# GpSimd's low halves of the weights: one subtraction over 512 columns, or two over 256

## The chip, the cores and the metric

The kernel runs on one NeuronCore of a Trainium2 chip. The metric is device microseconds for one execution, lower is better. Three runs of the kernel before took 1372.89, 1378.55 and 1378.11 us; the median is 1378.11 us. The profile is of one further execution.

## The reference

One sequence of 512 tokens with 1024 features goes through two different layers, all in float32.

- The first layer projects the normalised tokens with one wide matrix `w_in` into the inputs of three branches and three gates. Branch A is attention that keeps for each query 128 keys chosen by an index score; branch B is a gated linear recurrence (`hgrn2`); branch C is attention over compressed keys and values with rotary parts (`mla`). Each branch is projected up, gated, summed, projected by `w_out` and added to x. A feed-forward block with 2816 hidden columns follows: `x + (silu(h @ w_ffn_gate) * (h @ w_ffn_up)) @ w_ffn_down`, and a norm.
- The second layer scales and shifts its normalised input by a vector made from `c @ w_ada`, projects it with a second `w_in`, runs sparse attention of two branches with compressed keys beside them, and a state-space scan (`s5`), and adds the projected result to x.

Nearly all arithmetic is products of the tokens with weight matrices. Each weight is used once, so each is brought in from memory once per execution.

## The kernel before, in words

**Weights in two halves.** TensorE multiplies in a rounded float32. To keep full precision each operand is kept as two tiles, a high half (the value rounded) and a low half (what the rounding left), and one product is three matmuls: high by high, high by low, low by high. That is `mm3` (L176 to L179), and its three lines lead the profile. The halves of the activations are made by `split` (L181): a cast on ScalarE and a subtraction on VectorE. The halves of the weights are made by `wsplit` (L201): ScalarE casts the raw weights to `whi` (L206), and GpSimd subtracts, `wlo = wraw - whi` (L207).

**One load.** `wraw` (L194) brings up to 1024 float32 columns on 128 partitions (512 KB) into one of three raw buffers; the transfer is issued by SyncE's queue (L198). `wsplit` handles a load in two pieces, each of half of the load's `kc` blocks of rows: mostly 512 columns each, but 256 for the half-size loads, 64 to 384 for a few others, and 656 for two. There are three `whi` and three `wlo` buffers too. A raw buffer comes free, and the next transfer into it may start, when GpSimd has finished with it. A `whi` buffer comes free when the last matmul and the subtraction have read it. `early` (L131) asks for the next load one step before the present one is used.

**Who reads the low halves.** Where the weights are TensorE's stationary operand (`proj_t`, `proj_g`) the low half is read at L178; where they are the moving one (`proj_tok`, `proj_tok_g`) at L179. No other line changes with the piece of the subtraction.

**What sets the order.** Each engine works through its own list in order, and semaphores hold an instruction until what it reads is there. In the first stage the lists of TensorE, VectorE and ScalarE are in the order in which the code writes them (`manual_schedule`, L497). In all other stages the framework's planner orders each engine's list when the program is built, from its own estimate of when each instruction could start; a few edges (`issue_after`) pin single groups behind others. The code itself interleaves work by generators: the `todo` queue (L104) and `turns` (L140) step projections between the pieces of attention, the scan and the norms. GpSimd's list holds the subtractions of L207, and among them a few other things: the softmax weights (L365), masks for branch A (L1060, L1061), two products of a rotary table (L1650, L1651), and sums near the end.

**VectorE's chains that the prediction follows.** `rsqrt_steps` (L271) is a chain of eleven tiny operations on a few columns (L279 to L290). `rope2` (L1643) turns a tile by a table; copies at L1700 and transposes at L1704 follow. In the feed-forward loop (L1400) an activation is gated at L1406 and L1408 and split at L188, and between them VectorE makes the tables of the state-space scan (`cmul`, L1098, by `tt`, L1095). L838 adds a gated product to `mixed`.

Of the kernel before, what the change touches and what calls it, by code (L numbers as in the profile page):

```python
# [19 lines left out]
OP = mybir.AluOpType  # L20
# [72 lines left out]
def fl(ap):  # L93
    return ap.bitcast(FT)
# [56 lines left out]
def tile_hybrid(ctx: ExitStack, tc: tile.TileContext, I, out):  # L151
    nc = tc.nc
# [37 lines left out]
    def wload(parts, kc, cols, dst=None):  # L190

        return wsplit(wraw(parts, kc, cols), kc, cols, dst)
# [8 lines left out]
    def wsplit(raw, kc, cols, dst=None):  # L201
        hi, lo = dst or [wp.tile([128, 1024], FR, tag=t_, bufs=3, name=t_) for t_ in ("whi", "wlo")]
        n = kc * cols
        for c in range(0, kc, (kc + 1) // 2):
            d = slice(c * cols, min(c + (kc + 1) // 2, kc) * cols)
            nc.scalar.copy(hi[:, d], raw[:, d])  # L206
            nc.gpsimd.tensor_tensor(lo[:, d], raw[:, d], fl(hi[:, d]), op=OP.subtract)  # L207
        return [x[:, :n].rearrange("p (k c) -> p k c", k=kc) for x in (hi, lo)]

    def wcols(w, c0, cols, kc=KD, k0=0):  # L210
# [286 lines left out]
    with tc.manual_schedule(engines={mybir.EngineType.DVE, mybir.EngineType.Activation, mybir.EngineType.PE}):  # L497
# [13 lines left out]
        def weights(k):  # L511
            w_first[k] = wsplit(raws[k], min(3, KD - k), 328)
# [53 lines left out]
        for c0, n in ((0, 512), (512, 128)):  # L566
            p = s_ps()
            nc.tensor.matmul(p[0:4, 0:n], rb, oh[:, c0:c0 + n], start=True, stop=True)
            nc.scalar.copy(byd[:, c0:c0 + n], p[0:4, 0:n])
        half(2, 4)  # L570
        wk = wsplit(raw_k, KD, 128, [pa.tile([128, 1024], FR, name=f"wik{i}") for i in range(2)])
        product(0, 6)
        product(1, 6)
# [1508 lines left out]
```

## Time and profile before

| | |
|---|---|
| Median of three runs | 1378.11 us |
| The profiled execution: its own time | 1378.97 us |
| The profiled execution: span from first to last instruction | 1377.2 us |
| TensorE busy | 1279.4 us (93%) |
| VectorE busy | 858.9 us (62%) |
| GpSimd busy | 640.1 us (46%), of it 507.1 us in the 388 subtractions into `wlo` |
| ScalarE busy | 551.5 us (40%) |
| Mean granted TensorE clock | 0.97 of full speed |

In the views PE is TensorE's matmuls, PEld its weight loads, DVE is VectorE, ACT is ScalarE, POOL is GpSimd and SP is SyncE; a q behind an engine's name means its sequencer. A tile's name stands as written<-read. A busy time counts overlapping instructions once. A wait is put down to the release that came last.

### The profile page before, as it was taken

How to read it: one execution, taken by the hardware profiler on the slowest of the kernel's cores; microseconds unless marked ns; L12 is line 12 of the kernel's file. 1: busy time of each engine (PE TensorE's matmuls, PEld its weight loads, DVE VectorE, ACT ScalarE, POOL GpSimd, SP SyncE). 2: the span in 40 equal slices, each digit the busy share in tenths (PEclk: the TensorE clock that was granted, in tenths of full speed). 3: DMA queues.
4: the chain of work that ended last, by engine and by line, in shares of the span. 5: the costliest groups of instructions: out<-in, count | busy, mean ns of one | idle time of the engine just before them, and what ended most of it. 6: DMA issues, size and time to landing. Idle time of an engine off the chain costs nothing. (4 is left out here: it accounts for less than half of the span.)

```text
span 1377.2 us, 18201 instructions
## 1 busy us (share of the span) xinstructions
PE 1279.4 (93%) x6418; PEld 1054.0 (77%) x6418; DVE 858.9 (62%) x1831; ACT 551.5 (40%) x1242; POOL 640.1 (46%) x552
## 2 busy tenths in 40 slices
PE   8989999999989999999998899999989788789998
PEld 6777887777768888878876688887778678677786
DVE  6755897776534346268667516354363758897885
ACT  4554542322234434343423123432343234447772
POOL 3334433333455455554565345554532443547663
PEclk9999999999999999999999899999999898999999
DMA  6252222221423373333765434533325665231233
GB/s 199 71 158 58 63 75 65 62 57 36 116 80 88 86 176 92 123 92 115 224 196 187 143 99 121 169 109 102 113 77 162 185 173 132 69 92 47 77 108 138
DMA packets 201962, 156.16 MB, mean 113 GB/s; under 512 B 27535, under 2 KB 175707, under 8 KB 201869
## 3 DMA queue, kind: packets, MB, share of 16 engines
q1 hardware_dynamic: 201868, 154.98, 38.7%
q8 instruction: 51, 0.84, 0.3%
q14 instruction: 43, 0.34, 0.1%
HBM read 136.58 MB, written 18.37 MB: 113 GB/s over the span
## 5 line engine op out<-in xcount | busy, mean ns | idle before, releaser
L207 POOL TENSOR_TENSOR wlo<-wraw,whi 128x512 fp32r<-128x512 f32 (+4 forms) x388 | 507.1, 1327 | 602.7 <-ACT whi L206 601.4
L206 ACT CAST whi<-wraw 128x512 fp32r<-128x512 f32 (+4 forms) x388 | 212.3, 575 | 366.1 <-issue 217.3
L177 PE MATMUL mm<-hT,whi 128*128 128x512 f32 (+2 forms) x840 | 335.8, 400 | 0.0
L179 PE MATMUL mm<-hT,wlo 128*128 128x512 f32 (+2 forms) x840 | 327.9, 390 | 0.0
L178 PE MATMUL mm<-hT,whi 128*128 128x512 f32 (+2 forms) x840 | 327.7, 390 | 0.0
L179 PEld LDWEIGHTS mm<-hT,wlo 128*128 128x128 f32 x840 | 160.4, 191 | 31.3
L177 PEld LDWEIGHTS mm<-hT,whi 128*128 128x128 f32 x840 | 160.9, 191 | 29.9 <-PE mm L179 0.5
L178 PEld LDWEIGHTS mm<-hT,whi 128*128 128x128 f32 x840 | 161.0, 192 | 28.5 <-issue 0.7
L177 PE MATMUL mm<-whi,gT 128*128 128x512 f32 x176 | 71.7, 408 | 14.5 <-DVE t2k L1406 6.9
L1225 DVE TENSOR_TENSOR XT<-XT,mm 128x512 f32<-128x512 f32 x24 | 16.3, 685 | 99.7 <-PE mm L179 99.6
L178 PE MATMUL mm<-wlo,gT 128*128 128x512 f32 x176 | 71.3, 405 | 0.0
L179 PE MATMUL mm<-whi,gT 128*128 128x512 f32 x176 | 71.2, 405 | 0.0
L177 PE MATMUL mm<-whi,hT 128*128 128x512 f32 (+3 forms) x160 | 60.1, 375 | 0.3 <-ACT hT L184 0.3
L179 PE MATMUL mm<-whi,hT 128*128 128x512 f32 (+3 forms) x160 | 59.3, 371 | 0.9 <-DVE hT L185 0.9
L178 PE MATMUL mm<-wlo,hT 128*128 128x512 f32 (+3 forms) x160 | 59.3, 371 | 0.2 <-POOL wlo L207 0.2
L1287 DVE SCALAR_TENSOR_TENSOR am<-aw,prm,am 128x1024 f32<-128x1024 f32 x21 | 32.4, 1543 | 36.2 <-DMA aw<-in_w_ada_dram 36.2
L185 DVE TENSOR_TENSOR pt4k<-tp,pt4k 128x512 fp32r<-128x512 f32 (+1 forms) x96 | 45.8, 483 | 14.4 <-ACT pt4k L184 13.7
L177 PEld LDWEIGHTS mm<-whi,gT 128*128 128x128 f32 x176 | 34.2, 194 | 24.7 <-DVE t2k L1406 7.3
L184 ACT CAST pt4k<-tp 128x512 fp32r<-128x512 f32 (+1 forms) x96 | 40.1, 421 | 32.0 <-PE tp L387 30.8
L187 ACT ACTIVATE gT<-t2k 128x512 fp32r<-128x512 f32 x22 | 13.9, 631 | 82.3 <-DVE t2k L1408 82.3
L179 PEld LDWEIGHTS mm<-whi,gT 128*128 128x128 f32 x176 | 34.1, 194 | 8.3
L178 PEld LDWEIGHTS mm<-wlo,gT 128*128 128x128 f32 x176 | 34.1, 194 | 7.9
(641 smaller groups left out, 2666.8 us busy)
## 6 DMA issues: line engine op xcount, KB each, us to landing
wraw<-in_w_in_dram SPq DMA_DIRECT2D x70, 512.0 KB
aw<-in_w_ada_dram SPq DMA_DIRECT2D x24, 512.0 KB
wraw<-in_w_ffn_gate_dram SPq DMA_DIRECT2D x22, 512.0 KB
wraw<-in_w_ffn_up_dram SPq DMA_DIRECT2D x22, 512.0 KB
wraw<-in_w_ffn_down_dram SPq DMA_DIRECT2D x20, 512.0 KB
wraw<-in_w_out_dram SPq DMA_DIRECT2D x16, 512.0 KB
PA<-biasd SPq DMA_DIRECT2D x4, 640.0 KB
x<-in_x_dram SPq DMA_DIRECT2D x4, 512.0 KB
```

The source lines that it names most:

```text
L177: nc.tensor.matmul(o, a[0], b[0], start=first, stop=False)
L178: nc.tensor.matmul(o, a[0], b[1], start=False, stop=False)
L179: nc.tensor.matmul(o, a[1], b[0], start=False, stop=last)
L184: nc.scalar.copy(hi, p)
L185: return nc.vector.tensor_tensor(lo, p, fl(hi), op=OP.subtract)
L187: nc.scalar.activation(hi, p, AF.Copy, scale=scale)
L206: nc.scalar.copy(hi[:, d], raw[:, d])
L207: nc.gpsimd.tensor_tensor(lo[:, d], raw[:, d], fl(hi[:, d]), op=OP.subtract)
L1225: nc.vector.tensor_tensor(XT[:, t, n0:n0 + 512], XT[:, t, n0:n0 + 512], o, op=OP.add)
L1287: nc.vector.scalar_tensor_tensor(am, aw, cs[:, k:k + 1], am, op0=OP.mult, op1=OP.add)
```

## The change

The subtraction of each piece is issued in parts of at most 256 columns. The cast on ScalarE keeps its size, and the values written are the same. A piece of 512 columns becomes two instructions on GpSimd, one of 384 becomes 256 and 128, one of 656 becomes three; pieces of 256 and less stay as they are.

```diff
         for c in range(0, kc, (kc + 1) // 2):
             d = slice(c * cols, min(c + (kc + 1) // 2, kc) * cols)
             nc.scalar.copy(hi[:, d], raw[:, d])
-            nc.gpsimd.tensor_tensor(lo[:, d], raw[:, d], fl(hi[:, d]), op=OP.subtract)
+
+            for e0 in range(d.start, d.stop, 256):
+                e = slice(e0, min(e0 + 256, d.stop))
+                nc.gpsimd.tensor_tensor(lo[:, e], raw[:, e], fl(hi[:, e]), op=OP.subtract)
         return [x[:, :n].rearrange("p (k c) -> p k c", k=kc) for x in (hi, lo)]
```

## Rows read from the trace of the kernel before

**Rows 1.** The page: span, busy time of each engine, and the chain that ended last.
```profile
span 1377.2 us, 18201 instructions
...
PE 1279.4 (93%) x6418; PEld 1054.0 (77%) x6418; DVE 858.9 (62%) x1831; ACT 551.5 (40%) x1242; POOL 640.1 (46%) x552
...
PE 17%; DVE 8%; issue 1%; ACT 1%; DMA 1%; POOL 0%; DVEq 0%; SPq 0%; ACTq 0%; POOLq 0%
```

**Rows 2.** TensorE's waits: who waited for whom: us in total, times, longest us.
```profile
PE tp L1040 <- DVE rq_y L290: 8.8, 4, 6.1
...
PE tp L1704 <- DVE t2k L1700: 7.4, 2, 4.2
PE mm L177 <- DVE t2k L1406: 6.9, 1, 6.9
...
PE s L1012 <- DVE bK L1021: 3.7, 4, 1.7
...
PE mm L179 <- POOL wlo L207: 1.4, 1, 1.4
...
PE s L408 <- DVE mn L354: 0.2, 1, 0.2
```

**Rows 3.** GpSimd's groups by shape: count, busy us, mean ns, idle before, releaser.
```profile
L207 POOL TENSOR_TENSOR wlo<-wraw,whi 128x512 fp32r<-128x512 f32 x301 | 431.1, 1453 | 464.5 <-ACT whi L206 464.2
...
L207 POOL TENSOR_TENSOR wik<-wraw,wik 128x512 fp32r<-128x512 f32 x2 | 2.5, 1290 | 5.1 <-ACT wik L206 5.1
...
L1651 POOL TENSOR_TENSOR t2k<-tok,tab 128x256 f32<-128x256 f32 x2 | 1.5, 730 | 0.0
```

**Rows 4.** VectorE's groups by shape, two of the same shape.
```profile
L838 DVE TENSOR_TENSOR mixed<-mixed,t2k 128x512 f32<-128x512 f32 x16 | 21.4, 1335 | 0.3
...
L837 DVE SCALAR_TENSOR_TENSOR t2k<-t2k,mm 128x512 f32<-128x512 f32 x16 | 11.0, 687 | 41.2 <-PE mm L179 39.8 <-ACT t2k L835 1.4
```

**Rows 5.** Timeline of VectorE and GpSimd near 101 us: start us, duration us, instruction.
```profile
101.31 0.16 DVE L290 SCALAR_TENSOR_TENSOR rq_y<-rq_u,rq_y 128x4 f32<-128x4 f32 x1
101.51 1.21 DVE L286 TENSOR_TENSOR rq_u<-rq_y 128x4 f32<-128x4 f32 x1
...
101.44 1.26 POOL L207 TENSOR_TENSOR wlo<-wraw,whi 128x512 fp32r<-128x512 f32 x1 [1.17 <-ACT whi L206]
```

**Rows 6.** The same near 261 us, where GpSimd's pieces have 256 columns.
```profile
260.78 0.70 DVE L290 SCALAR_TENSOR_TENSOR rq_y<-rq_u,rq_y 128x4 f32<-128x4 f32 x1
...
260.73 1.55 POOL L207 TENSOR_TENSOR wlo<-wraw,whi 128x256 fp32r<-128x256 f32 x2 [7.77 <-ACT whi L206]
```

**Rows 7.** The same from 1169 to 1177.5 us.
```profile
1170.86 1.51 DVE L1653 TENSOR_TENSOR tok<-tok,tab 128x256 f32<-128x256 f32 x1
...
1176.38 0.89 DVE L1700 COPY t2k<-tok 128x256 f32<-128x256 f32 x4
...
1170.62 5.69 POOL L207 TENSOR_TENSOR wlo<-wraw,whi 128x512 fp32r<-128x512 f32 x4
```

**Rows 8.** The same from 752 to 760.5 us.
```profile
757.58 1.24 DVE L1096 TENSOR_TENSOR t2k<-PH 128x8 f32<-128x8 f32 x1
...
759.36 0.68 DVE L1406 SCALAR_TENSOR_TENSOR t2k<-t2k,mm 128x512 f32<-128x512 f32 x1
...
751.62 7.17 POOL L207 TENSOR_TENSOR wlo<-wraw,whi 128x512 fp32r<-128x512 f32 x4 [4.31 <-ACT whi L206]
```

**Rows 9.** Waits of ScalarE and of SyncE's queue.
```profile
ACT whi L206 <- PE mm L178: 80.1, 39, 6.3
ACT whi L206 <- POOL wlo L207: 34.9, 18, 4.2
...
SPq L198 <- POOL wlo L207: 843.8, 165, 15.7
```

**Rows 10.** One stretch: busy us of PE, PEld, DVE, ACT, POOL; granted clock; DMA.
```profile
760.00:766.00 6.00, 2.68 (x6) 1.67 (x7) 5.79 (x27) 0.63 (x1) 0.00 (x0) 0.50 0.46 132
```

**Rows 11.** Timeline of GpSimd alone: two pieces of 512 columns back to back.
```profile
776.95 2.54 POOL L207 TENSOR_TENSOR wlo<-wraw,whi 128x512 fp32r<-128x512 f32 x2 [2.08 <-ACT whi L206]
```

## The prediction

> **What bounds the kernel now.** I read the page's busy times first: TensorE is busy 1279.4 of 1377.2 us, VectorE 62%, GpSimd 46% [rows 1]. So at most 98 us are idle on TensorE, and whatever the change does off TensorE is worth nothing until it touches those. The chain of waits agrees: TensorE 17% of the span, VectorE 8%, GpSimd 0% (the chain is followed back only part of the way) [rows 1]. Next, the list of TensorE's waits, to see who ends the idle time. The 26 entries of that list that VectorE ends run from 8.8 us down to 0.2 us [rows 2] and add up to 78 us; GpSimd's subtraction ends almost nothing directly, 1.4 us in its largest entry [rows 2]. The low halves are therefore early enough, and the question is whether GpSimd reaches TensorE by way of VectorE.
>
> It does. L838 and L837 are both 128x512 on VectorE; L837 reads PSUM (`mm`) and takes 687 ns, L838 reads two SBUF tiles and takes 1335 ns on the mean [rows 4]. The timeline shows why. At 101.31 us a step on 4 columns takes 0.16 us. The next begins at 101.51, just after a subtraction began at 101.44, and takes 1.21 us: it ends at 102.72, when the subtraction (to 102.70) is done [rows 5]. With pieces of 256 columns the same kind of step takes 0.70 us [rows 6]. So a VectorE operation on SBUF waits for the rest of the running subtraction, 1.21 − 0.16 = 1.05 us behind 512 columns and 0.54 behind 256.
>
> **The change part by part.**
>
> *The instructions.* 327 pieces have 512 columns: 301 into `wlo` [rows 3] and 26 into four other tiles. They become 654; the odd widths (384, 328, 280, 656) add 28 more. So GpSimd gets 355 more. An undisturbed subtraction of 512 columns takes 1290 ns; a two-input operation on 256 takes 730 [rows 3]. Two for one cost 2 × 730 − 1290 = 170 ns, over 327 pieces 56 us, and some 5 us for the odd ones: GpSimd goes from 640 to about 700 us, 51%. By spacing: two of 512 take 2.54 us together, 1.27 each [rows 11], two of 256 1.55 us with some waiting [rows 6], which gives 0 to 0.28 us per pair; I keep 0.17. The Trainium skill (Perfetto Trace Analysis, GPSIMD Engine Instruction) says to time GpSimd by the spacing of starts, since its spans don't compose; by the spacing with waits, 0.28, the added work would be 92 us, still below any engine's limit.
>
> *What hides it.* TensorE's work on a load hides the subtraction. The cast waits 80.1 us in 39 places for TensorE to free its buffer [rows 9], so in these places the weights run ahead by the depth of the buffers. If that cover is gone, a stall per load grows by two to four times 0.17. The next transfer is issued when GpSimd frees the raw buffer: SyncE waits 843.8 us for that, 165 times [rows 9], so each of these transfers goes out 0.3 us later, behind it in SyncE's queue everything else too. ScalarE waits for GpSimd 34.9 us, 18 times [rows 9]; with two late pieces each, 18 × 0.34 = 6 us, and behind the waiting cast stand the evictions that VectorE waits for. ScalarE is 40% busy, so I cost this at 0, with 6 us as the upper bound. TensorE may start a load after its first 256 columns of low half, which is worth at most the 1.4 us it waits now [rows 2]; I take 0.
>
> *What VectorE gains.* A single operation that meets a subtraction waits half as long: 0.5 us less behind a full piece, 0.25 on the mean. A chain of operations is another matter. VectorE and GpSimd then alternate, one instruction each, until the burst of subtractions is used up. I worked two chains that end in a stall.
>
> First, 1170.86 to 1176.38 us: four operations in step with four subtractions of 512, 5.52 / 4 = 1.38 us apart, then the copies, two of which release TensorE [rows 7]. With pieces of 256 the step shrinks by 1290 − 730 = 0.56 to 0.82 us, but eight pieces stand ahead, so the two copies queue as well: 6 × 0.82 = 4.9 us, against 5.52 plus some 0.4 for the copies. Gain: 1.0 of the 4.2 us stall [rows 2].
>
> Second, the stall of 6.9 us before 760 us. The burst of four runs from 751.62 to 758.79; a last operation waits in it, on 8 columns, from 757.58, and L1406 starts at 759.36 behind four more tiny ones [rows 8]. With eight pieces those tiny ones get in step too: each pays about 0.5 us until the burst ends, and the burst itself is 4 × 0.17 = 0.7 longer. Loss: about 0.5 us.
>
> So where the chain outlasts the burst nothing is won and 0.17 per piece is lost; where it needs something before the burst is over, it wins 0.5 per operation.
>
> *The sum.* Short waits behind one or two operations (like the entry of 3.7 us in 4 times on L1012 [rows 2]): some 20 waits, of which I take 0.3 each: −6. The dozen waits above 2 us: between −1.0 and +0.5 each by the two chains worked; I take −0.2, so −2. The clock: after the 6.9 us stall TensorE's granted clock is 0.50 in the stretch from 760 to 766 us, its lower level [rows 10]; 3 us were lost there. A stall that shrinks enough would spare some of that; I take one third of one such stretch, −1. Together −9. Bounds: if every short wait is halved and every long one gains 1.0, −6 − 12 − 6 = −24; if every chain outlasts its burst, +13 (below). The profiled execution took 1378.97 us, 0.06% above the median of 1378.11 us; 1378.97 − 9 = 1370 us.
>
> **The rivals.**
>
> *The port only changes hands more often (slower).* VectorE's wait is GpSimd's time, and GpSimd's time grows. For: the second chain; a step in the rsqrt chain pays 1.05 behind one of 512 and twice 0.54 behind two of 256, in which nothing is won [rows 5, 6]. It decides wherever a chain has as many SBUF operations left as the burst has pieces. Price: about 13 waits above 2 us, each behind a burst of four: 13 × 4 × 0.19 = 10 us, with one more stretch of 6 us at half clock, 3 us: 1392 us. Against: L838 waits alone, behind L837, in the middle of bursts [rows 4], and there half of the wait goes. The Trainium skill (SBUF — State Buffer, Who interferes with whom) speaks for it: a VectorE operation with two SBUF inputs and a GpSimd operation that reads SBUF lock each other out for the whole instruction. By that the total is conserved, and only a place in the queue is won.
>
> *VectorE gains, but off the path.* TensorE is busy 93% [rows 1], most VectorE operations have slack, and L838 releases nothing that TensorE is waiting for. Then the short waits shrink by little: −1 to −3, 1377 us. For: no entry of TensorE's waits [rows 2] is ended by L838, the group with the most waiting. Against: 78 us of TensorE's idle time end with VectorE.
>
> *The planner lays the lists out anew.* 355 more instructions on GpSimd move its estimate of when each load is ready, so lists after the first stage may come out in another order. One stall like that of 6.9 us with its 3 us of clock [rows 2, 10] may vanish or arise: 1369 or 1389 us, with no sign to expect. That the change doesn't do what it says I rule out: the pieces are plain in the code.
>
> **How the numbers follow.** Forecast (1370): 0.50. Port only changes hands (1392): 0.20. Off the path (1377): 0.20. Planner (1369 or 1389): 0.10. About 0.5%, 7 us, can be told from no change, so faster is below 1371 and slower above 1385. The forecast's own range is 1356 to 1377, and sums near −9 fall on both sides of 1371: 0.36 faster, 0.14 no change. Off the path: 0.02, 0.16, 0.02. Port: 0.02 no change, 0.18 slower. Planner: 0.05 and 0.05. Together faster 0.43, same 0.32, slower 0.25. The range reaches from 1356 (−24 is 1355) to 1391, short of the full price of the slower rival and of a stall that arises beside it.
>
> **What would show it.** Right: L838's mean falls from 1335 to about 1000 ns; VectorE's busy time falls by 20 us or more while GpSimd's rises to about 700; the waits of TensorE on L1012 and L1704 shrink, those on L1406 don't. The slower rival would show VectorE's busy time unchanged, and the long waits of TensorE each 0.7 us longer. Off the path: VectorE's busy time falls and TensorE's idle time stays at 98 us. The planner: lines in another order on VectorE or ScalarE around a stall. The prediction is wrong if GpSimd or ScalarE ends more than some 10 us of TensorE's waits, that is, if the cover of the loads was thinner than I read it.

## The result, and the profile after

The kernel with pieces of 256 columns takes 1353.83 us (median of 4 runs, 1351.87 to 1355.84) against 1378.33 us before (4 runs): a ratio of 0.983, 95% interval 0.9806 to 0.9854. The sign was forecast, the size was not: 24.5 us where the sum said 9, and 2 us below the range.

In the code of after, everything behind the edited loop stands three lines further down (L838 is L841, L1700 is L1703), and the subtraction is L210. First the page of after: span, busy times, and the shares of the chain.

```profile
span 1350.1 us, 18698 instructions
...
PE 1270.3 (94%) x6418; PEld 1045.1 (77%) x6418; DVE 831.6 (62%) x1831; ACT 551.3 (41%) x1242; POOL 720.4 (53%) x907
...
PE 17%; DVE 8%; issue 1%; ACT 1%; POOL 0%; DVEq 0%; ACTq 0%; POOLq 0%
```

Against [rows 1]: the same 6418 matmuls, 355 more instructions on GpSimd and 80 us more of its time, 27.3 us less on VectorE, 27.1 us less of span. TensorE's own busy time fell by 9.1 us although it does the same work. TensorE, ScalarE and VectorE issue their instructions in the same order as before (on VectorE but for two memsets), so nothing was laid out anew. (The two profiled executions took 1378.97 and 1351.87 us, so they lie 27.1 us apart where the medians lie 24.5; the account below is of the 27.1.)

The next two fences are groups by shape. GpSimd's main group, which answers to [rows 3]:

```profile
L210 POOL TENSOR_TENSOR wlo<-wraw,whi 128x256 fp32r<-128x256 f32 x687 | 571.9, 860 | 504.7 <-ACT whi L206 503.7
```

VectorE's two operations of [rows 4]:

```profile
L841 DVE TENSOR_TENSOR mixed<-mixed,t2k 128x512 f32<-128x512 f32 x16 | 16.1, 1004 | 0.3
...
L840 DVE SCALAR_TENSOR_TENSOR t2k<-t2k,mm 128x512 f32<-128x512 f32 x16 | 11.0, 687 | 43.3 <-PE mm L179 41.9 <-ACT t2k L838 1.4
```

The one that reads two tiles in SBUF went from 1335 to 1004 ns; the one that reads PSUM stayed at 687. The rsqrt steps of [rows 5], in the timeline of after:

```profile
97.87 0.16 DVE L289 TENSOR_TENSOR rq_u<-rq_y 128x4 f32<-128x4 f32 x1
98.07 0.58 DVE L291 SCALAR_TENSOR_TENSOR rq_u<-rq_u,rq_v 128x4 f32<-128x4 f32 x1
98.69 0.65 DVE L293 SCALAR_TENSOR_TENSOR rq_y<-rq_u,rq_y 128x4 f32<-128x4 f32 x1
...
97.91 1.40 POOL L210 TENSOR_TENSOR wlo<-wraw,whi 128x256 fp32r<-128x256 f32 x2 [0.88 <-ACT whi L206]
```

Where one step stood 1.21 us behind a piece of 512, two steps now stand 0.58 and 0.65 us behind two of 256. Last, TensorE's waits (us in total, times, longest), against [rows 2]:

```profile
PE tp L1043 <- DVE rq_y L293: 8.2, 4, 5.9
PE tp L1707 <- DVE t2k L1703: 8.1, 4, 3.3
PE mm L177 <- DVE t2k L1409: 7.0, 1, 7.0
...
PE tp L1737 <- DVE t2k L1733: 3.6, 1, 3.6
...
PE s L1015 <- DVE bK L1024: 1.6, 3, 0.6
PE mm L179 <- POOL wlo L210: 1.3, 1, 1.3
```

One entry of before that is needed here and below:

```profile
PE tp L1734 <- DVE t2k L1730: 7.9, 2, 7.0
```

L1015 (L1012 before) went from 3.7 to 1.6 us; L1409 (L1406) stayed at 7.0; L1737 (L1734, 7.9 us before) is down to 3.6; L1707 (L1704) rose from 7.4 to 8.1, in four waits in place of two; GpSimd still ends next to nothing.

**The account.** After its first matmul TensorE was idle for 88.5 us before and is for 70.8 after: −17.6. Its busy time fell by 9.1, and it starts 0.3 us sooner: together the 27.1 us of span. The trace's record of the granted clock sums to 84.5 us at the half clock before and 58.2 after. Within these stretches TensorE was busy 64.9 us before and is for 46.2 after; half of that difference is 9.3 us, so this is where the 9.1 us come from.

I paired TensorE's instructions of the two traces one by one and sorted its waits by their length before. Forty short places fell from 29.2 to 23.1 us, fourteen places with a wait above 2 us from 58.6 to 44.5, and six new ones cost 2.5. The short ones gave 6, as the sum had it, but that is partly luck: it had some 20 places at 0.3 us each, and there were 40 at 0.15. The long ones gave 14 where it had 2, and the clock 9 where it had 1; the new waits took 2.5 back.

### The profile page after: what moved, and what is told of

Same layout as the page of the kernel before. It is cut to its first block, busy times and chain, and to the rows that moved or that the text cites. A ratio compares the mean times of both kernels' runs of the same rounds, so it can differ in the third digit from the quotient of the medians.

```text
span 1350.1 us, 18698 instructions
## 1 busy us (share of the span) xinstructions
PE 1270.3 (94%) x6418; PEld 1045.1 (77%) x6418; DVE 831.6 (62%) x1831; ACT 551.3 (41%) x1242; POOL 720.4 (53%) x907
## 5 line engine op out<-in xcount | busy, mean ns | idle before, releaser
L210 POOL TENSOR_TENSOR wlo<-wraw,whi 128x256 fp32r<-128x256 f32 (+2 forms) x717 | 581.9, 841 | 506.9 <-ACT whi L206 506.0
L178 PE MATMUL mm<-hT,whi 128*128 128x512 f32 (+2 forms) x840 | 326.4, 389 | 0.0
L178 PEld LDWEIGHTS mm<-hT,whi 128*128 128x128 f32 x840 | 160.2, 191 | 28.3 <-issue 0.7
L178 PE MATMUL mm<-wlo,gT 128*128 128x512 f32 x176 | 70.5, 400 | 0.0
L178 PE MATMUL mm<-wlo,hT 128*128 128x512 f32 (+3 forms) x160 | 58.5, 365 | 0.3 <-POOL wlo L210 0.3
L178 PEld LDWEIGHTS mm<-wlo,gT 128*128 128x128 f32 x176 | 33.7, 191 | 7.9
```

Source lines behind the costliest of these rows:

```text
L178: nc.tensor.matmul(o, a[0], b[1], start=False, stop=False)
L210: nc.gpsimd.tensor_tensor(lo[:, e], raw[:, e], fl(hi[:, e]), op=OP.subtract)
```

## The experiments

All times are medians, ratios to the kernel before (1375.0 to 1375.6 us in these series, 1378.3 for after). The table also has TensorE's idle time after its first matmul, its time at the half clock, and the busy times, all in us and from the profiled executions.

| kernel | time | ratio, 95% | idle | half clock | TensorE | VectorE | GpSimd |
|---|---|---|---|---|---|---|---|
| before | 1378.3 | 1 | 88.5 | 84.5 | 1279.4 | 858.9 | 640.1 |
| after | 1353.8 | 0.983 [0.981, 0.985] | 70.8 | 58.2 | 1270.3 | 831.6 | 720.4 |
| p256_rev | 1351.8 | 0.983 [0.981, 0.985] | 70.6 | 62.3 | 1271.6 | 832.6 | 722.9 |
| first_part | 1363.6 | 0.993 [0.990, 0.995] | 78.8 | 64.2 | 1270.9 | 836.4 | 684.9 |
| p128 | 1339.0 | 0.973 [0.971, 0.976] | 61.7 | 42.4 | 1267.5 | 794.4 | 856.8 |
| p96 | 1362.6 | 0.991 [0.988, 0.994] | 75.4 | 69.2 | 1276.8 | 786.6 | 971.6 |
| p64 | 1403.7 | 1.021 [1.019, 1.023] | 100.3 | 109.2 | 1291.8 | 820.5 | 1083.0 |
| memset512 | 1268.9 | 0.923 [0.921, 0.925] | 15.6 | 1.5 | 1242.2 | 710.5 | 287.5 |
| copy512 | 1291.3 | 0.940 [0.938, 0.943] | 29.4 | 16.8 | 1249.2 | 741.8 | 372.1 |
| fill | 1374.6 | 0.999 [0.997, 1.001] | 81.2 | 69.4 | 1284.5 | 858.4 | 639.1 |
| dve512 | 1319.1 | 0.960 [0.957, 0.962] | 43.4 | 47.4 | 1263.3 | 934.2 | 102.6 |
| mix_half | 1322.8 | 0.961 [0.960, 0.963] | 51.1 | 41.0 | 1262.3 | 878.6 | 513.2 |
| p128_all | 1344.6 | 0.977 [0.975, 0.979] | 62.1 | 53.7 | 1273.1 | 791.9 | 870.1 |
| dve512_all | 1306.0 | 0.949 [0.948, 0.951] | 36.7 | 38.4 | 1258.2 | 923.3 | 125.6 |

**p256_rev: is it the shorter hold, or an earlier start?** With two pieces TensorE may also begin on the first 256 columns sooner. Issued from the back, the columns that TensorE needs first are ready last:

```diff
-            for e0 in range(d.start, d.stop, 256):
+            for e0 in reversed(range(d.start, d.stop, 256)):
```

> Pieces of 256 columns, issued from the last columns to the first: each GpSimd instruction is as short as in the kernel after, but the columns that TensorE multiplies first are ready last, as with one subtraction over 512. Theory 'held port': as fast as the kernel after, 1354 us (ratio 0.983, between 0.980 and 0.986), idle time of TensorE about 71 us. Rival 'early start' (the gain comes from TensorE starting on the first 256 columns before the second 256 are there): the gain is gone, 1375 to 1382 us (ratio 0.997 to 1.003), idle about 88 us. A mixture lies between.

It took 1351.8 us, ratio 0.983, with 70.6 us idle: the kernel after. The earlier start is worth nothing here, as the prediction costed it.

**first_part: is the gain local?**

Against the kernel before, with `...` where lines are left out:

```diff
+    seen = []
...
+        n, _ = kc * cols, seen.append(1)
...
+            st = 256 if len(seen) <= 125 else 512
+            for e0 in range(d.start, d.stop, st):
+                e = slice(e0, min(e0 + st, d.stop))
```

> Pieces of 256 columns for the first 125 loads of weights only (those used up to about 630 us), pieces of 512 after that. Theory 'local stalls': each stall that is shortened gives its time where it stands, and half-clock stretches vanish only behind those stalls; the lead over the kernel before grows to about 12 us by 600 us, as in the kernel after, and then stays: 1366 us (ratio 0.991, between 0.988 and 0.994); half-clock time 84 -> about 73 us. Rival 'swallowed': the lead is lost again at later waits for transfers, 1373 or more. Rival 'one place decides': nearly the whole gain or none of it, 1355 or 1378.

1363.6 us, ratio 0.9925, as expected; the half-clock time fell to 64.2 us where about 73 was expected. The profile shows the two halves apart. TensorE's waits of this kernel:

```profile
PE tp L1737 <- DVE t2k L1733: 7.8, 2, 6.9
PE tp L1707 <- DVE t2k L1703: 7.5, 2, 4.3
PE s L411 <- DVE qst L188: 4.0, 1, 4.0
PE s L411 <- DVE iqs L185: 1.1, 1, 1.1
```

The wait on `iqs`, at 48 us, is 1.1 us as in after (2.9 before). The other three lie beyond 1000 us and are what they were before: 6.9 (7.0), 4.3 (4.2) [rows 2] and 4.0 (3.6). Each of these waits answers to the pieces in its own neighbourhood, and what is won early is not lost later: in the profiled execution (1360.12 us, the fastest of the four) the lead over before is 13.5 us at 600 us, 18.0 at 1000 and 18.8 at the end (the medians lie 11.7 us apart).

**p128, p96 and p64: how far does it go?**

```diff
-            for e0 in range(d.start, d.stop, 256):
-                e = slice(e0, min(e0 + 256, d.stop))
+            for e0 in range(d.start, d.stop, 128):
+                e = slice(e0, min(e0 + 128, d.stop))
```

and so with 96 and 64. TensorE, VectorE and ScalarE keep the order of after in all three.

> Pieces of 128 columns instead of 256, everything else as in the kernel after; the lists of TensorE, VectorE and ScalarE stay in the same order. Theory 'held port': VectorE waits out the rest of the running GpSimd instruction, so a still shorter instruction takes off about half of what the step from 512 to 256 took off: TensorE's idle time 71 -> about 62 us, time about 1342 us (ratio to the kernel before 0.974), VectorE's busy time down by 10 to 20 us more. Rival 'hand-overs': each piece adds a fixed cost and another turn at the port; VectorE's busy time stays or rises, GpSimd goes beyond 850 us, and the time is 1354 us or more (ratio 0.983 to 0.998). Rival 'early start' (TensorE may begin on the first columns of a low half sooner): a small gain, 1350.

> Pieces of 96 columns (512 columns are five of 96 and one of 32), between 128 (1339 us) and 64 (1404 us); the lists stay as they are. By the pieces measured (0.31 us over 64, 0.44 over 128) one over 96 takes about 0.38, so 512 columns take 5 x 0.38 + 0.24 = 2.1 us and a load of 1024 columns 4.3 us, against 5.5 us of TensorE's work on it; GpSimd's busy time comes to some 960 us. Theory 'GpSimd as the bound turns it': it is not reached yet on the mean, but the stages with the densest loads already wait; 1335 to 1350 us (ratio 0.971 to 0.982), TensorE's waits on low halves between the 7.7 us at 128 and the 26 us at 64. Rival 'held port alone': the waits of VectorE fall on, 1330 us.

> Pieces of 64 columns. Theory 'held port': a wait of VectorE behind one piece falls from 0.28 us (the mean behind pieces of 128) to about 0.18, and with no subtraction at all TensorE's idle time was 15.6 us against 61.7 here, so there is still something to take: about 1330 us (ratio 0.967). Rival 'GpSimd becomes the bound': a subtraction over 64 columns took 0.31 to 0.41 us, so 1024 columns take 5.0 us and more, against 5.5 us that TensorE needs for them; GpSimd's busy time goes past 1000 us, TensorE waits for low halves, and the time is 1339 us or more. Rival 'hand-overs': VectorE's busy time no longer falls below the 794 us of the kernel with pieces of 128.

128 columns go on as the held port has it: ratio 0.973, VectorE 37 us less busy. Then it turns, at 96 already: 0.991, and 1.021 at 64. GpSimd's main groups show one reason; first 128, then 96, then 64:

```profile
L210 POOL TENSOR_TENSOR wlo<-wraw,whi 128x128 fp32r<-128x128 f32 x1388 | 705.0, 543 | 374.0 <-ACT whi L206 373.6
```

```profile
L210 POOL TENSOR_TENSOR wlo<-wraw,whi 128x96 fp32r<-128x96 f32 x1707 | 720.2, 453 | 300.4 <-ACT whi L206 300.1
...
L210 POOL TENSOR_TENSOR wlo<-wraw,whi 128x32 fp32r<-128x32 f32 x301 | 98.2, 326 | 0.0
```

```profile
L210 POOL TENSOR_TENSOR wlo<-wraw,whi 128x64 fp32r<-128x64 f32 x2784 | 922.4, 374 | 240.3 <-ACT whi L206 240.2
```

By these means, 512 columns of low half cost GpSimd 1.45 us before [rows 3], 2 × 0.860 = 1.72 in after, 4 × 0.543 = 2.17 at 128, 5 × 0.453 + 0.326 = 2.59 at 96 and 8 × 0.374 = 2.99 at 64. TensorE multiplies 512 columns of weights in 12 matmuls; in the trace of before they start 0.227 us apart where it runs through (748.04 to 751.67 us, 16 steps), so 2.72 us. At 64 GpSimd is slower than that. TensorE's waits of p64 (us in total, times, longest):

```profile
PE mm L178 <- POOL wlo L210: 18.0, 12, 3.5
...
PE s L178 <- POOL ex L210: 4.7, 7, 0.9
```

GpSimd's low halves now end 18.0 us of waits on L178 alone where it was 4.0 at 128. There is a second reason, on the side of the rival 'hand-overs': at 64 VectorE's waits did not fall to 0.18 us, and its busy time rose. VectorE's group L841 in p64, and its longest case with GpSimd's line beside it in the timeline:

```profile
L841 DVE TENSOR_TENSOR mixed<-mixed,t2k 128x512 f32<-128x512 f32 x16 | 32.6, 2039 | 0.3
```

```profile
546.78 4.99 DVE L841 TENSOR_TENSOR mixed<-mixed,t2k 128x512 f32<-128x512 f32 x1
...
545.77 6.92 POOL L210 TENSOR_TENSOR wlo<-wraw,whi 128x64 fp32r<-128x64 f32 x21
```

The operation takes 0.69 us when nothing holds it; here it stood 4.3 us while sixteen pieces went by, each about 0.31 us, one right behind the other. Twenty of VectorE's waits in p64 lasted for six pieces or more and make up most of its waiting. At 96 there are five waits of 1.5 to 1.8 us behind five or six pieces; at 128 none is behind more than two. L841's mean goes 1335, 1004, 824, 808 and 2039 ns from 512 columns to 64. Why VectorE does not get in between the short pieces no run shows.

At 96 the mean leaves 0.13 us of room, but TensorE already waits 7.8 us on L178, and the kernel is 24 us slower than with 128. My expectation of 1335 to 1350 was too good: I had set GpSimd's mean time against TensorE's, and the mean does not show the stages in which the loads come densest. Of the other 10 us of idle time at 96, the 6.0 at `xb` (0.8 at 128) come from GpSimd too, by way of ScalarE: one cast there waits 8.3 us for GpSimd's subtraction into `ex`, a wait that p128 does not have, and the cast of `xb` stands behind it. The rest (7.1 us at L1409 where it was 5.1, and smaller ones) was not taken apart.

**memset512 and copy512: what does the port cost in all?** In the first GpSimd only writes, in the second it reads one input. Neither subtracts. Against the kernel before:

```diff
-            nc.gpsimd.tensor_tensor(lo[:, d], raw[:, d], fl(hi[:, d]), op=OP.subtract)
+            nc.gpsimd.memset(fl(lo[:, d]), 0.0)             # memset512
+            nc.gpsimd.tensor_copy(lo[:, d], fl(hi[:, d]))   # copy512
```

> GpSimd writes zeros over each 512 columns of the low half in place of subtracting (it leaves out the low halves' values; it reads nothing, and does not wait for ScalarE's cast). A memset of 512 columns took 0.53 us in the profile, about as long as a subtraction over 256. Theory 'any GpSimd instruction holds VectorE': about as the kernel after, 1350 to 1356 us, VectorE's operations still stand for some 0.5 us behind the memsets. Theory 'only instructions that read SBUF hold VectorE': the waits behind the subtractions vanish, VectorE's busy time falls from 832 to below 720 us, TensorE's idle time below 62 us, time 1330 to 1342 us (ratio 0.965 to 0.974). Rival 'early start': the low halves are there before the high ones, so the gain would be large too, but VectorE's busy time would not fall.

> GpSimd copies each 512 columns of the high half into the low half (it leaves out the subtraction; the third product then uses the high half twice), so that it reads one input in SBUF, writes one output, and waits for ScalarE's cast as before. Theory 'two inputs hold the port': as with the memsets, VectorE's busy time about 710 us, TensorE's idle time below 25 us, 1265 to 1285 us (ratio 0.92 to 0.935). Theory 'any reading instruction holds VectorE': a copy takes about 0.75 us, between the subtractions over 256 (0.74) and the memset; VectorE waits some 0.4 us behind each, about 1340 to 1356 us (0.975 to 0.985). Rival 'early start' (the memset's gain came from low halves that were there before the high ones): 1300 us or more with VectorE's busy time at 710.

1268.9 us: 106 us below before, far beyond what I expected of the memsets. (In these two kernels TensorE's list comes out in another order in 70 of 6418 places, all behind 1150 us; by 1100 us the memsets' lead over before is already 81 us.) VectorE's group L841 tells it; memset512:

```profile
L841 DVE TENSOR_TENSOR mixed<-mixed,t2k 128x512 f32<-128x512 f32 x16 | 11.0, 690 | 0.3
```

690 ns is the time of its neighbour on PSUM, 687: nothing of the 648 ns of waiting [rows 4] is left. Nor is it the low halves' being there early: copy512 waits for ScalarE's cast as before and still takes 1291.3, between the ranges of both theories. There a wait behind a copy of 512 columns (0.73 us) is left, L841 at 826 ns, and TensorE is idle 13.8 us longer than with the memsets. So a GpSimd instruction that reads one input holds VectorE too, for its shorter time; my line between one input and two was wrong. The Trainium skill (SBUF — State Buffer, Who interferes with whom) draws it elsewhere: VectorE with two SBUF inputs contends with a GpSimd instruction that reads SBUF, not with one that only writes it. The two runs agree with that. Copies and TENSOR_SCALAR operations, with one input in SBUF, are held as well, and by memsets too: set against the shortest operation on the same tiles, 12 of the 14 of them that began while a memset ran stood over 0.15 us, and none of some eighty with two inputs in SBUF.

**fill: does the clock follow the stall?** Into the kernel before, between the matmuls that stand around TensorE's waits of 6.9 and 3.2 us near 760 us (the call there has `fill={2: 28, 3: 13}`):

```diff
+            if fill and k == 0 and t in fill:
+                z = tp_ps()
+                for _ in range(fill[t]):
+                    nc.tensor.matmul(z[:, :cols], x[0][:, 0, 0:128], w[0][:, 0, :cols], start=True, stop=True)
```

> The kernel before, with 41 more matmuls of 128x512 whose results nothing reads: 28 in TensorE's wait of 6.9 us (from 753.2 us on, ended by VectorE's L1406) and 13 in the wait of 3.2 us right behind it (ended by L1408). The lists are otherwise the same and the two waits stay as long. Theory 'the clock falls behind a stall': the 13.65 us at the half clock that begin near there vanish, and the kernel is about 6 us faster though it does 41 matmuls more (1369 us, ratio 0.995); the matmuls after 760 us run at 0.23 us each instead of 0.43. Rival 'the clock falls by its own calendar': the half-clock stretch stays, and the time is the same or longer by what the added matmuls overshoot (ratio 1.000 to 1.002).

The same stretches as [rows 10], before and then with the filling (busy us of PE, PEld, DVE, ACT, POOL; granted clock; DMA):

```profile
766.00:772.00 6.00, 6.00 (x21) 4.79 (x20) 4.19 (x9) 1.14 (x2) 0.65 (x1) 0.75 0.50 154
```

```profile
760.00:766.00 6.00, 5.10 (x22) 3.83 (x21) 5.79 (x26) 0.63 (x1) 0.00 (x0) 1.00 0.41 132
766.00:772.00 6.00, 6.00 (x28) 4.82 (x27) 4.22 (x7) 1.15 (x2) 2.61 (x2) 1.00 0.50 175
```

The clock stays at 1.00 where it was 0.50 and 0.75, so this half-clock stretch came with TensorE's standing still. The gain of 6 us did not come: the ratio cannot tell it from nothing, and matmul by matmul the lead over before grows from 1.31 us (at 752.84 us) to 2.70 (at 769.24) across the place. Of the 13.65 us at the half clock only the matmuls behind the second wait counted, at 0.43 us in place of 0.23: there the lead grows by 1.8 us, after 0.45 had been lost up to the end of that wait. During the rest TensorE was waiting for VectorE anyway.

**dve512, mix_half, p128_all and dve512_all: is there a better place for the work?** All low halves on VectorE; half of each load there; GpSimd's other two-input operations in smaller pieces too (the sums of 128 columns, the rotary products of 256 and 64); and the first with the third. Single lines of the four changes, with `...` between them:

```diff
+            nc.vector.tensor_tensor(lo[:, d], raw[:, d], fl(hi[:, d]), op=OP.subtract)   # dve512, dve512_all
...
+            eng, st = (nc.vector, 512) if c == 0 else (nc.gpsimd, 128)                   # mix_half
...
-        nc.gpsimd.tensor_tensor(P[:, 128:], P[:, 128:], selm, op=OP.add)
+        [nc.gpsimd.tensor_tensor(P[:, x:x + 128], P[:, x:x + 128], selm[:, x - 128:x], op=OP.add)
+         for x in range(128, 1280, 128)]           # p128_all, dve512_all, and so at four other places
```

> VectorE makes the low halves itself, one subtraction over 512 columns at some 0.68 us, and GpSimd none; the planner lays the lists out anew. Theory 'held port': nothing holds VectorE any more, its busy time is 710 us (as with the memsets) plus 343 x 0.68 = 233, so about 945 us or 72% of the span, and what TensorE waits for is VectorE's longer list: between 1300 and 1345 us. Rival 'VectorE becomes the bound': each piece of the chain waits behind subtractions of 0.68 us as it did behind GpSimd's, 1345 to 1400 us.

> VectorE subtracts for the first half of each load (one operation over 512 columns, 0.70 us), GpSimd for the second half in pieces of 128; the planner lays the lists out anew. With all low halves on VectorE it took 1319 us at 934 us of VectorE's time, with all on GpSimd in pieces of 128 it took 1339 at 794. Theory 'held port': half of the pieces, so half of the waits behind them (54 us in place of 108) and half of the added operations (112 us): VectorE at about 710 + 54 + 112 = 876 us, time between the two or a little below, 1310 to 1330. Rival 'both prices are paid': the waits come where VectorE is now fuller, 1330 to 1350.

> Pieces of 128 columns for the subtraction and also for GpSimd's other operations with two inputs (the mask sum over 1152 columns, the two rotary products over 1024, the sums and products over 512 near the end); the lists of TensorE and VectorE stay in order. In the kernel with pieces of 128 some ten of VectorE's operations still stood behind these, 11 us in all, single ones for 1.1 to 2.2 us. Theory 'held port': where such a wait lies in a chain that TensorE waits for, it shrinks to 0.3 us: 2 to 5 us less than 1339, about 1335 (ratio 0.971). Rival 'off the path': no change, 1339 (0.973).

> The low halves on VectorE, as in the kernel at 1319 us, and GpSimd's other operations with two inputs in pieces of 128 columns; the lists stay as in that kernel. There some 14 operations of VectorE still stood behind GpSimd's long ones, 17 us in all. Theory 'held port': TensorE's waits of 4.6 us behind VectorE's rsqrt steps (the mask sum over 1152 columns runs there) and of 4.7 us in the rotary stage shrink by 1 to 2 us each: 1312 to 1317 us (ratio 0.955). Rival 'off the path': 1319 (0.9595).

VectorE does the subtractions itself at 0.70 us each, is busy 934 us, and the kernel takes 1319.1 us: 20 us less than the best split on GpSimd. Sharing them (1322.8) gains nothing on it. The planner laid out the lists of these kernels anew (TensorE's differs from that of before in 862 of 6418 places in dve512 and dve512_all, in 487 in mix_half), and how much of their gain is owed to that no run shows; dve512 and dve512_all have the same order. With GpSimd's other operations cut up as well it is 1306.0 us, ratio 0.949, the best of all here, and 13 us better than dve512 where I expected 2 to 7. TensorE's waits of dve512, then of dve512_all:

```profile
PE tp L1043 <- DVE rq_y L293: 4.8, 2, 4.6
PE tp L1707 <- DVE t2k L1703: 4.7, 1, 4.7
```

```profile
PE tp L1707 <- DVE t2k L1703: 3.6, 2, 2.4
```

The wait behind the mask sum over 1152 columns (L1043) has left the head of the list, the rotary one (L1707) fell to 3.6. The same cutting on top of p128 went the other way, 1344.6 in place of 1339.0 us (ratios 0.977 and 0.973, whose intervals still overlap by a little), which neither theory had; its TensorE is idle no longer (62.1 us), but 11 us longer at the half clock, in waits that came out in another distribution. Whether the loss is real and where it comes from is open.

## Why the forecast had the sign and not the size

**The mechanism stands.** VectorE waits out the running GpSimd instruction. With each VectorE operation set against the shortest of its form, 163 of them stood over 0.15 us behind a piece of 512 before, 0.92 us on the mean; 267 behind a piece of 256 in after, 0.52 us; 380 behind 128, 0.28 us. The sums are 149.6, 139.9 and 107.9 us. Before also has some 26 such waits behind narrower pieces, about 14 us, so all its waits come to about 164 us, and some 24 of them are gone in after; VectorE's busy time, which fell by 27.3 us, says much the same. The rest of the waiting, six sevenths of it, was dealt out anew, as the slower rival said. How much TensorE gets of what is saved depends on where in VectorE's list it lies; the step below is about that.

Two things are narrower than the prediction had them. Not every VectorE operation on SBUF is held: of those that began in before while a subtraction went on for over 0.15 us, some 150 of 195 with two inputs in SBUF stood, all 6 copies and 19 of 28 TENSOR_SCALAR, but none of 42 RECIPROCAL, MAX8, MATCH_REPLACE8 and TENSOR_REDUCE, and none of some 140 that read PSUM. And VectorE and GpSimd do not always alternate, one instruction each: in p64 sixteen pieces went ahead of one operation (above), and below VectorE passes a piece four times in a row.

**What held.** L838's mean was forecast at about 1000 ns and is 1004; VectorE's busy time at 20 us less or more, and is 27.3 less; GpSimd's at about 700, and is 720 (its pieces wait for VectorE too). The waits on L1406 were to stay and stayed; those on L1012 were to shrink and did. The sum on L1704 was to shrink too, and rose from 7.4 to 8.1 us: its two old waits got shorter (4.2 to 3.3, 3.2 to 1.6), but one of 0.8 us came right behind the first and one of 2.4 us at 1187.7 us, where there was 0.1 before. The cover of the loads held: of TensorE's idle time VectorE ends 58.7 us in place of 78.3, ScalarE 8.8 in place of 7.7, GpSimd 2.9 in place of 2.0. The slower rival is out (VectorE's busy time fell), off the path is out (idle fell by 17.6), the planner is out (same order).

Both worked chains went much as worked. In the second the tiny operations in front of L1406 get in step with the smaller pieces, as said; timeline of after, against [rows 8]:

```profile
742.78 0.70 DVE L1099 TENSOR_TENSOR t2k<-PH 128x8 f32<-128x8 f32 x1
743.51 0.65 DVE L1099 TENSOR_TENSOR PH<-PH,t2k 128x8 f32<-128x8 f32 x1
...
744.87 0.67 DVE L1099 TENSOR_TENSOR PH<-PH,t2k 128x8 f32<-128x8 f32 x1
745.46 0.68 DVE L1409 SCALAR_TENSOR_TENSOR t2k<-t2k,mm 128x512 f32<-128x512 f32 x1
```

The wait went from 6.87 to 7.0 us, a loss of 0.1 where 0.5 was worked out. In the first (1170.86, [rows 7]) the wait of 4.22 us fell to 3.29, a gain of 0.9 against 1.0. But of the four copies that queue there the chain had counted two, and the other two make the new wait of 0.8 us, so little is left of that gain.

**The step that failed: "I take −0.2, so −2" for the dozen waits above 2 us.** It measured −14.1. Both chains were worked inside the stall or just ahead of it, and there the answer was right: over the fifteen single waits above 2 us, which fell by 14.9 us together, VectorE won next to nothing between the beginning of the wait and its end: 0.5 us, if its lead is taken at the last operation that it had ended when TensorE stopped, −1.9 if at the next one that it began. What it had won before TensorE began to wait adds up to 14.5 or 16.9 (at that moment, VectorE's lead over the kernel before, less TensorE's). A wait of TensorE is the lateness of VectorE's whole list since VectorE itself last waited, and I had cut the list where TensorE stopped.

The wait of 7.0 us on L1734, which fell to 3.6, shows it. TensorE stands still from 1087.2 to 1094.2 us before and from 1068.7 to 1072.3 in after. VectorE's last wait of its own ends at 1076.9, and at 1059.4 in after. From there, in the timeline of before:

```profile
1076.89 2.27 DVE L1730 COPY t2k<-tok 128x256 f32<-128x256 f32 x2 [0.61 <-ACT tok L1682]
...
1081.17 1.12 DVE L1559 TENSOR_TENSOR_SCAN W<-R,W 128x256 f32<-128x256 f32 x1
1082.21 1.43 DVE L1513 TENSOR_TENSOR W<-W,t2k 128x256 f32<-128x256 f32 x1
1083.56 1.51 DVE L1565 TENSOR_TENSOR t2k<-W,PH 128x252 f32<-128x252 f32 x1
1084.99 1.78 DVE L1559 TENSOR_TENSOR_SCAN W<-R,W 128x256 f32<-128x256 f32 x1
...
1092.86 0.85 DVE L1568 TENSOR_TENSOR S<-t2k 64x252 f32<-64x252 f32 x2
1093.72 0.29 DVE L1730 COPY t2k<-tok 128x256 f32<-128x256 f32 x1
```

and the same operations in after:

```profile
1059.41 1.18 DVE L1733 COPY t2k<-tok 128x256 f32<-128x256 f32 x2 [0.61 <-ACT tok L1685]
...
1062.75 0.67 DVE L1562 TENSOR_TENSOR_SCAN W<-R,W 128x256 f32<-128x256 f32 x1
1063.35 0.39 DVE L1516 TENSOR_TENSOR W<-W,t2k 128x256 f32<-128x256 f32 x1
1063.66 0.40 DVE L1568 TENSOR_TENSOR t2k<-W,PH 128x252 f32<-128x252 f32 x1
1063.99 0.67 DVE L1562 TENSOR_TENSOR_SCAN W<-R,W 128x256 f32<-128x256 f32 x1
...
1069.73 1.70 DVE L1571 TENSOR_TENSOR S<-t2k 64x252 f32<-64x252 f32 x2
1071.45 0.72 DVE L1733 COPY t2k<-tok 128x256 f32<-128x256 f32 x1
```

The four operations from 1081.17 took 5.60 us from the first's start to the last's end and now take 1.91, and all four start ahead of TensorE's stop at 1087.2. A shorter hold alone does not explain that. Before, each of the four stood behind one subtraction of 512. In after GpSimd had pieces to do as well, but one of them stood for VectorE:

```profile
1062.73 2.47 POOL L210 TENSOR_TENSOR wlo<-wraw,whi 128x256 fp32r<-128x256 f32 x1
```

It began just ahead of the first of the four, takes 0.73 us when nothing holds it [rows 3], and ended at 1065.19, when the four had run one behind the other (to 1064.67). In p256_rev the piece there takes 2.46 us and the wait of 7.0 us is 3.6 as well, so this comes with pieces of 256; what decides who goes first no run shows. Behind the stop the pieces of 256 cost what the slower rival said: the two `S` operations went from 0.85 to 1.70, the last copy from 0.29 to 0.72.

**The second: the clock at −1.** It measured −9.1 us of TensorE's busy time, as the half-clock time fell by 26.3. Five of the fifteen half-clock stretches are gone, those at the waits that end at 48.3, 103.8, 713.3, 989.9 and 1229.6 us; they are 17.1 of the 26.3 us, and the rest is what others came out shorter or longer. Not all of this is firm: at 103.8 the wait only went from 2.94 to 2.68 us, and in p256_rev, with the same 2.68, the stretch is there again. The first, at 48.4 us before and at 46.3 in after:

```profile
48.40:52.00 3.60, 3.60 (x14) 3.60 (x15) 1.15 (x3) 1.30 (x3) 0.00 (x0) 0.56 0.30 98
```

```profile
46.30:49.90 3.60, 3.60 (x20) 3.11 (x21) 2.15 (x4) 2.27 (x5) 0.67 (x1) 1.00 0.45 129
```

In the same 3.6 us TensorE runs 20 matmuls instead of 14. I had read the clock off the longest stall, where TensorE waits on through the half clock and little is lost (filling it gave 1.8 us back where I had 3 as lost), and which the change leaves alone; a medium stall, at whose end it has work queued, can pay the whole stretch, as the one at 48.4 us does. Since the long waits were under-sized, so were the stretches that follow them.

The bound of −24, 1355 us, was made from the same two examples, and the result passes it by a microsecond.

## What to carry over

Where VectorE and GpSimd both read SBUF, size GpSimd's instructions by how long VectorE can afford to stand behind one, down to where GpSimd's time for a piece of data, waiting included, comes near what its reader needs for it (here 2.2 us of 2.7 was best, 2.6 was already too much), and see in the trace that VectorE still gets in between the pieces; or take the work off GpSimd, which was better still here, with the lists laid out anew. To price a change in an engine's waits, follow that engine's list back to its own last wait, not to the moment at which the bottleneck stopped. Count the clock with each stall that may vanish, but only for the matmuls that run at the half clock while nothing else is late.

## What the hardware showed unexpectedly

- The whole cost of GpSimd's reading: with memsets in place of subtractions TensorE's idle time is 15.6 us against 88.5, its clock 1.00 in the mean against 0.970, and the kernel takes 7.7% less time.
- A GpSimd copy of 512 columns with one input in SBUF still held 97 VectorE operations, for 0.38 us on the mean; a memset of 512 columns, 0.53 us long, held hardly any (15, for 0.35), and by the stricter count above only copies and TENSOR_SCALAR operations.
- At 64 columns VectorE stood 0.54 us on the mean behind pieces that take 0.37: with the pieces that small several go ahead of it in a row, up to sixteen, and its busy time rose again, from 786.6 us at 96 columns to 820.5.
- It goes the other way too: one piece of 256 columns took 2.47 us, while four VectorE operations went ahead of it.
- TensorE's idle time and its time at the half clock go together over the fourteen kernels, if not in step: from 15.6 and 1.5 us to 100.3 and 109.2.
